# Start addresses of TensorE's operands in SBUF, one encoder layer on one core

## The chip, the cores and the metric

The kernel runs on one core of a Trainium2 chip. The metric is the device time of one launch in microseconds (us); lower is better. Engines are named as in the profile: PE is TensorE's matmul, PEld its weight load, DVE is VectorE, ACT is ScalarE, SP issues the DMAs.

## The reference

One layer of an encoder on 512 tokens with 1024 features, float32. With `rms` for a normalization over the features with a gain, it computes

```
h = x + 0.5 * rms(ffn1(rms(x)))          ffn(u) = (silu(u @ Wg) * (u @ Wu)) @ Wd, inner size 2816
h = h + rms(mixer(rms(h)))               mixer: w_in -> q, k, v, pool, two gates; attention over a
                                         neighbourhood of an 8 x 64 grid, pooling with four windows,
                                         each projected, gated and added, then w_out
h = h + 0.5 * rms(ffn2(rms(h)))
h = h + rms((p @ Wp) * sigmoid(rms(h) @ Wgate))
```

## The kernel before

Features lie on the 128 partitions and tokens along the row, so an activation is eight tiles of 128 x 512. Every float32 value is kept as a high part rounded to fp32r and a low remainder. `mm3` makes one product of a 128 x 128 weight block out of three matmuls: high weight by high activation (L277), high weight by low activation (L278), low weight by high activation (L279). In each, the weight block is the stationary operand (read by PEld) and the activation the moving one.

Weights arrive in chunks of 128 x 1024 words (class `Stream`). A chunk is loaded by SP into a ring of five `raw` tiles, split by ACT (high part, L243) and DVE (low part, L165) into one of six `w` tiles, and freed when PE has used it. `pump` works up to `SPLIT_AHEAD` = 4 chunks ahead. A `w` tile is 2176 words wide, 128 more than its two halves need, so that the halves can begin at a shift, in words, that depends on the kind of the chunk (`self.shift`); the low half lies 1088 words behind the high one, which is a multiple of 256 bytes. `plan()` gives the kind: 0 for products of 512 columns, 1 for groups that are done in two halves of 256 tokens (first and last groups of a stage, so that norms can overlap), 2 for quads.

A quad (`fast_group`) makes two row blocks of gate and up projections with seven products of half size in place of eight, each of 24 matmuls with 256 columns, into three PSUM banks p, q and r. Product i takes its moving operands from `moving(i, k)`: products 0, 1 and 6 from the normalized input `uh`, `ul`, products 3 and 4 from the combined inputs x0 to x3, products 2 and 5 from x4 to x7. `xtile(n)` says where the combined input n is kept: x0 to x3 in the tiles of tag y, x4 and x5 in tags pth and ptl, x6 and x7 in tag e. Each of the two FFNs has three parts (`PARTS`): a first part with groups 0 to 2 in 512 columns, and two parts of four quads; each part ends with its down projection. So there are four stages of four quads.

The order of instructions is written out by hand: a list of Python generators with due times (`Clock`, `TIMES`) places norms, attention and pooling between the matmuls. The change touches none of these times.

Tiles lie one behind another in each pool, every row rounded up to 32 bytes, and tags in the order of their first use; that is why some tags are taken once, early, with nothing written. In the memory map of the compiled program the starts modulo 256 bytes are:

```
tiles                                                       pool    start mod 256
h, uh, ul, acc, rb, and tags f, y, zh0, zh1, zl0, zl1       act     0
rc_pre (16 bytes)                                           tmp     0
pth, ptl, e                                                 tmp     32
w tiles (six, 8704 bytes each)                              wsp     0; operands at 4 x shift:
    kind 0                                                          0
    kind 1, and quads but for i = 2, 5                              64
    quads, i = 2, 5                                                 96
```

All offsets inside these tiles at which a matmul begins are multiples of 256 bytes.

Of the kernel before, what the change touches and what calls it, by code (L numbers as in the profile page):

```python
# [10 lines left out]
F32 = mybir.dt.float32  # L11
F32R = mybir.dt.float32r
# [3 lines left out]
P = 128  # L16
S = 512
# [4 lines left out]
NT = 4  # L22
# [96 lines left out]
def kernel(  # L119
# [16 lines left out]
    act = ctx.enter_context(tc.tile_pool(name="act", bufs=1))  # L136
    tmp = ctx.enter_context(tc.tile_pool(name="tmp", bufs=2))
# [33 lines left out]
    class Stream:  # L171
# [5 lines left out]
        def __init__(self):  # L177
            self.ops = []
            self.needs = []
            self.shift = []  # L180
            chunk = 0
            for kind in plan():
                quad = kind == 2
                for i in range(7 if quad else 1):
                    self.ops.append((quad, chunk, i))
                    self.needs.append(chunk + (self.LOADS[i] if quad else 1))
                    self.shift.append(24 if quad and i in (2, 5) else 16 if kind else 0)
                chunk += 4 if quad else 1
            self.n = len(self.ops)
            assert chunk == n_chunks  # L190
            self.loaded = 0
            self.split = 0
            self.done = 0
            self.hold = False
            self.freed = set()
            self.over = set()
            self.raw = {}
            self.parts = {}
            self.both = None
# [95 lines left out]
    G1PRE, G1POST, GMPRE, GMPOST, G2PRE, G2POST, GPPRE, GPPOST = (gain(v) for v in range(8))  # L295
    pscale = [g_sb[:, 64 + g:65 + g] for g in range(4)]

    h = [act.tile([P, S], F32, name=f"h{k}") for k in range(KD)]
    uh = [act.tile([P, S], F32R, name=f"uh{k}") for k in range(KD)]
    ul = [act.tile([P, S], F32R, name=f"ul{k}") for k in range(KD)]  # L300
    acc = act.tile([P, S], F32, name="acc")
    rb = act.tile([P, S], F32, name="rb")

    rc_pre = tmp.tile([P, NT], F32, name="rc_pre", bufs=1)
    for tag, bufs in (("pth", 2), ("ptl", 2), ("e", 4)):
        tmp.tile([P, S], F32, tag=tag, name=tag, bufs=bufs)

    def u_rhs(k):
        return uh[k], ul[k]
# [191 lines left out]
    def ffn(chains, gpre, gpost, gnext):  # L501
# [21 lines left out]
        def combined():  # L523

            for k in range(4):
                a, b = un[k], un[k + 4]
                tt(a[:, LEFT], a[:, LEFT], a[:, RIGHT], ALU.subtract)
                tt(a[:, RIGHT], a[:, RIGHT], b[:, RIGHT], ALU.subtract)
                stt(b[:, RIGHT], a[:, LEFT], -1.0, b[:, RIGHT], ALU.mult, ALU.subtract)
                tt(b[:, LEFT], b[:, LEFT], b[:, RIGHT], ALU.add)  # L530
                for n, src in ((k, a), (k + 4, b)):
                    xh[n], xl[n] = xtile(n)
                    nc.scalar.copy(xh[n], src)
                    tt(xl[n], src, f32(xh[n]), ALU.subtract)
                yield TIMES["comb"]

        def xtile(n):
            if n < 4:
                return [act.tile([P, S], F32R, tag="y", name="x", bufs=8) for _ in range(2)]
            if n < 6:  # L540
                return [tmp.tile([P, S], F32R, tag=t, name="x") for t in ("pth", "ptl")]
            return [tmp.tile([P, S], F32R, tag="e", name="x", bufs=4) for _ in range(2)]

        def moving(i, k):
# [505 lines left out]
def plan():  # L1050

    def ffn(first):
        out = []
        for g0, g1 in PARTS:
            for g in range(g0, g1):
                out += [2] if g in FAST else [first if g == 0 else 0] * 4
            out += [0] * (g1 - g0) + [int(g1 == PARTS[-1][1])] * (g1 - g0)
        return out

    mixer = [1] * 4 + [0] * (3 * 4 + 1 + 16 + 8 + 4) + [1] * 4  # L1060
    return ffn(0) + mixer + ffn(1) + [0] * 3 + [1] * 8
# [114 lines left out]
```

## Time and profile before

| | |
|---|---|
| median of three runs | 1081.99 us (1080.77 to 1083.11) |
| the profiled execution | 1084.12 us, its span 1082.3 us |
| PE busy | 1060.2 us, 6762 matmuls |
| DVE busy, ACT busy | 762.3 us, 544.2 us |
| HBM read | 104.93 MB |

The span is the time from the first to the last instruction of one profiled execution; the execution's own time holds a little more at both ends. A matmul's duration in a row includes its way through the array and overlaps the next one's, so the pace of a run of matmuls is read from one start to the next.

### The profile page before, as it was taken

The numbers are of one execution on the slowest core, as the hardware profiler recorded it, in microseconds if no ns is written. First come the engines' busy times: TensorE is split into PE (matmuls) and PEld (weight loads), VectorE is DVE, ScalarE is ACT, GpSimd is POOL, SyncE is SP. The second block draws the span as 40 slices with busy tenths as digits, with TensorE's granted clock in tenths as the row PEclk, the third lists the DMA queues.
The fourth block names the chain that finished last, engine by engine and source line by source line (L and its number), as shares of the span: only waits on it lengthen the run. The fifth ranks groups of instructions, "written<-read, shape, count | busy, mean of one in ns | idle before, by whom it ended". The sixth has DMA issues, their size and how long they took to land.

```text
span 1082.3 us, 16827 instructions
## 1 busy us (share of the span) xinstructions
PE 1060.2 (98%) x6762; PEld 955.9 (88%) x6762; DVE 762.3 (70%) x1279; ACT 544.2 (50%) x921; POOL 0.7 (0%) x6
## 2 busy tenths in 40 slices
PE   9999999999999999999999999999999999999994
PEld 7788999889999988877888899888999889999894
DVE  7893787558854987977444429994787558854976
ACT  8552555235543765366222247752555235543874
POOL 0000000000000000000000000000000000000000
PEclk9999999999999999999999999999999999999997
DMA  8331335223362342231333321342235223341202
GB/s 297 107 104 59 87 109 157 78 78 104 111 178 50 108 153 79 78 98 45 99 96 95 97 76 40 107 133 72 81 115 155 79 79 100 109 162 60 63 17 79
DMA packets 37023, 108.12 MB, mean 100 GB/s; under 512 B 4816, under 2 KB 11472, under 8 KB 36944
## 3 DMA queue, kind: packets, MB, share of 16 engines
q1 hardware_dynamic: 36800, 107.01, 31.7%
q8 instruction: 53, 0.87, 0.3%
q14 instruction: 26, 0.21, 0.1%
q10 hardware_dynamic: 144, 0.03, 0.0%
HBM read 104.93 MB, written 2.10 MB: 99 GB/s over the span
## 4 chain that ended last, share of the span: by engine, by line
PE 90%; DVE 6%; ACT 3%; issue 0%; DMA 0%; DVEq 0%; ACTq 0%
PE g L277 14%; PE g L278 14%; PE g L279 14%; PE p L278 6%; PE p L279 6%; PE p L277 6%; PE r L278 3%; PE r L279 3%; PE r L277 3%; PE gate L279 2%; PE gate L277 2%; PE gate L278 2%; PE q L278 1%; PE q L279 1%; PE q L277 1%; PE br L277 1%
## 5 line engine op out<-in xcount | busy, mean ns | idle before, releaser
L165 DVE TENSOR_TENSOR w<-raw,w 128x1024 fp32r<-128x1024 f32 (+1 forms) x227 | 273.7, 1208 | 152.6 <-ACT w L243 152.4
L243 ACT CAST w<-raw 128x1024 fp32r<-128x1024 f32 (+1 forms) x227 | 234.7, 1038 | 262.1 <-PE g L279 131.5
L277 PE MATMUL g<-zh,w 128*128 128x512 f32 (+1 forms) x512 | 178.6, 349 | 0.0
L278 PE MATMUL g<-zl,w 128*128 128x512 f32 (+1 forms) x512 | 178.3, 348 | 0.0
L279 PE MATMUL g<-zh,w 128*128 128x512 f32 (+1 forms) x512 | 178.3, 348 | 0.0
L279 PE MATMUL g<-uh,w 128*128 128x256 f32 (+1 forms) x448 | 146.5, 330 | 1.4 <-DVE w L165 1.4
L278 PE MATMUL g<-ul,w 128*128 128x256 f32 (+1 forms) x448 | 147.4, 330 | 0.2 <-DVE ul L168 0.2
L277 PE MATMUL g<-uh,w 128*128 128x256 f32 (+1 forms) x448 | 146.4, 331 | 0.6 <-ACT w L243 0.6
L278 PEld LDWEIGHTS g<-zl,w 128*128 128x128 f32 x512 | 96.6, 189 | 12.4
L279 PEld LDWEIGHTS g<-zh,w 128*128 128x128 f32 x512 | 96.2, 188 | 12.6
L277 PEld LDWEIGHTS g<-zh,w 128*128 128x128 f32 x512 | 96.2, 188 | 12.4
L279 PEld LDWEIGHTS g<-uh,w 128*128 128x128 f32 x448 | 84.7, 190 | 9.7 <-DVE w L165 1.6
L278 PEld LDWEIGHTS g<-ul,w 128*128 128x128 f32 x448 | 85.4, 191 | 8.5 <-DVE ul L168 0.6
L277 PEld LDWEIGHTS g<-uh,w 128*128 128x128 f32 x448 | 84.8, 190 | 8.8 <-ACT w L243 0.9
L279 PE MATMUL p<-uh,w 128*128 128x256 f32 x256 | 71.9, 281 | 0.0
L278 PE MATMUL p<-ul,w 128*128 128x256 f32 x256 | 71.9, 281 | 0.0
L277 PE MATMUL p<-uh,w 128*128 128x256 f32 x256 | 71.9, 281 | 0.0
L278 PE MATMUL p<-x,w 128*128 128x256 f32 x256 | 71.5, 279 | 0.0
L278 PE MATMUL r<-x,w 128*128 128x256 f32 x256 | 71.5, 279 | 0.0
L279 PE MATMUL p<-x,w 128*128 128x256 f32 x256 | 71.5, 279 | 0.0
L279 PE MATMUL r<-x,w 128*128 128x256 f32 x256 | 71.4, 279 | 0.0
L277 PE MATMUL p<-x,w 128*128 128x256 f32 x256 | 71.4, 279 | 0.0
(195 smaller groups left out, 2187.6 us busy)
## 6 DMA issues: line engine op xcount, KB each, us to landing
raw<-in_wst SPq DMA_DIRECT2D x191, 512.0 KB, 3.6
h<-in_x SPq DMA_DIRECT2D x8, 256.0 KB, 5.5
bm<-in_bias SPq DMA_DIRECT2D x64, 32.0 KB, 2.2
out<-o SPq DMA_DIRECT2D x16, 128.0 KB, 1.7
raw<-in_wst SPq DMA_DIRECT2D x4, 128.0 KB, 4.0
g_sb<-in_gains ACTq DMA_DIRECT2D x1, 34.0 KB, 3.2
edge_sb<-in_edge SPq DMA_DIRECT2D x1, 32.0 KB, 5.3
```

Source lines behind the costliest of these rows:

```text
L165: nc.vector.tensor_tensor(o, a, b, op=op)
L243: nc.scalar.copy(hi[:, sl], raw[:, sl])
L277: nc.tensor.matmul(o, wh, xh, start=first, stop=False, **kw)
L278: nc.tensor.matmul(o, wh, xl, start=False, stop=False, **kw)
L279: nc.tensor.matmul(o, wl, xh, start=False, stop=last, **kw)
```

## The change

`rc_pre` moves from the pool tmp to the front of the pool act, where it takes eight words of a row. The early taking of tags in tmp is put in another order, with 56 words of padding ahead of pth. Both tiles of the combined input x4 are taken from tag pth, both of x5 from ptl. The shift of a weight chunk is 24 words for kinds 1 and 2 and 8 words for kind 0.

```diff
@@ class Stream, __init__
-                    self.shift.append(24 if quad and i in (2, 5) else 16 if kind else 0)
+                    self.shift.append(24 if kind else 8)
@@ tile_encoder_kernel
+    rc_pre = act.tile([P, 8], F32, name="rc_pre")[:, 0:NT]
     h = [act.tile([P, S], F32, name=f"h{k}") for k in range(KD)]
     uh = [act.tile([P, S], F32R, name=f"uh{k}") for k in range(KD)]
     ul = [act.tile([P, S], F32R, name=f"ul{k}") for k in range(KD)]
     acc = act.tile([P, S], F32, name="acc")
     rb = act.tile([P, S], F32, name="rb")
-
-    rc_pre = tmp.tile([P, NT], F32, name="rc_pre", bufs=1)
-    for tag, bufs in (("pth", 2), ("ptl", 2), ("e", 4)):
+    for tag, bufs in (("ptl", 2), ("e", 4)):
         tmp.tile([P, S], F32, tag=tag, name=tag, bufs=bufs)
+    tmp.tile([P, 56], F32, name="pad", bufs=1)
+    tmp.tile([P, S], F32, tag="pth", name="pth")
@@ ffn, xtile
             if n < 6:
-                return [tmp.tile([P, S], F32R, tag=t, name="x") for t in ("pth", "ptl")]
+                return [tmp.tile([P, S], F32R, tag="pth" if n == 4 else "ptl", name="x") for _ in range(2)]
```

## Rows read from the trace of the kernel before

**Rows 1.** The page's head and busy times: span, busy us, share, instructions.
```profile
span 1082.3 us, 16827 instructions
...
PE 1060.2 (98%) x6762; PEld 955.9 (88%) x6762; DVE 762.3 (70%) x1279; ACT 544.2 (50%) x921; POOL 0.7 (0%) x6
```

**Rows 2.** The page's chain that ended last, shares by engine.
```profile
PE 90%; DVE 6%; ACT 3%; issue 0%; DMA 0%; DVEq 0%; ACTq 0%
```

**Rows 3.** Stretches: length, busy of PE, PEld, DVE, ACT, POOL; clock, DMA, GB/s.
```profile
110.40:188.80 78.40, 78.40 (x673) 78.40 (x672) 62.29 (x71) 43.89 (x63) 0.00 (x0) 1.00 0.40 120
188.80:232.40 43.60, 43.60 (x194) 36.11 (x194) 21.67 (x24) 9.72 (x11) 0.00 (x0) 1.00 0.24 75
...
882.50:961.00 78.50, 78.50 (x674) 78.46 (x673) 64.16 (x74) 43.23 (x61) 0.00 (x0) 1.00 0.38 121
```

**Rows 4.** The same view, the first quad's products 0 to 3.
```profile
110.34:113.17 2.83, 2.83 (x25) 2.82 (x24) 1.05 (x1) 1.65 (x3) 0.00 (x0) 1.00 0.00 0
113.17:116.00 2.83, 2.83 (x26) 2.83 (x25) 1.22 (x2) 1.53 (x2) 0.00 (x0) 1.00 0.51 143
116.00:118.74 2.74, 2.74 (x26) 2.74 (x25) 2.27 (x4) 1.37 (x2) 0.00 (x0) 1.00 0.60 194
118.74:121.57 2.83, 2.83 (x26) 2.83 (x25) 2.34 (x3) 1.54 (x2) 0.00 (x0) 1.00 0.10 39
```

**Rows 5.** PE in order of time, product 2: start us, duration us, instruction.
```profile
116.01 0.28 PE L277 MATMUL p<-x,w 128*128 128x256 f32 x1
116.12 0.29 PE L278 MATMUL p<-x,w 128*128 128x256 f32 x1
116.25 0.28 PE L279 MATMUL p<-x,w 128*128 128x256 f32 x1
116.37 0.28 PE L277 MATMUL p<-x,w 128*128 128x256 f32 x1
...
118.63 0.28 PE L279 MATMUL p<-x,w 128*128 128x256 f32 x1
```

**Rows 6.** PE in order of time, two half groups, first and last of 97 and 39.
```profile
332.70 0.28 PE L277 MATMUL g<-zh,w 128*128 128x256 f32 x1
...
344.00 0.28 PE L277 MATMUL g<-zh,w 128*128 128x256 f32 x1
...
355.93 0.28 PE L277 MATMUL g<-uh,w 128*128 128x256 f32 x1
...
360.23 0.28 PE L279 MATMUL g<-uh,w 128*128 128x256 f32 x1
```

**Rows 7.** PE in order of time, a down projection: its begin, and later.
```profile
188.86 0.40 PE L277 MATMUL g<-zh,w 128*128 128x512 f32 x1
...
190.25 0.39 PE L277 MATMUL g<-zh,w 128*128 128x512 f32 x1
...
199.77 0.39 PE L277 MATMUL g<-zh,w 128*128 128x512 f32 x1
...
201.81 0.39 PE L277 MATMUL g<-zh,w 128*128 128x512 f32 x1
```

**Rows 8.** PE in order of time, the matmuls of pool_map and the next.
```profile
449.57 0.40 PE L277 MATMUL py<-ph,w 128*128 128x512 f32 x1
...
450.27 0.39 PE L277 MATMUL g<-uh,w 128*128 128x512 f32 x1
```

**Rows 9.** Groups by line and shape, 110.40 to 188.80, the split of weights.
```profile
L165 DVE TENSOR_TENSOR w<-raw,w 128x1024 fp32r<-128x1024 f32 x25 | 30.6, 1224 | 13.8 <-ACT w L243 13.8
L243 ACT CAST w<-raw 128x1024 fp32r<-128x1024 f32 x25 | 26.2, 1050 | 11.9 <-PE p L279 5.2 <-PE q L279 3.9 <-issue 2.8
```

**Rows 10.** DMA issues: KB each, median us from issue to landing.
```profile
h<-in_x SPq DMA_DIRECT2D x8, 256.0 KB, 5.5
```

## The prediction, made before the change was run

> **What bounds the kernel now.** I read the page's busy times first: TensorE (PE) is busy 98% of the 1082.3 us span and the next engine, DVE, 70% [rows 1]. The chain of work that ended last says the same from the other end: 90% of it is PE [rows 2]. So a matmul that starts sooner after the one before it shortens the run, unless something else then becomes late. The view of stretches shows where PE never stops: in a quad stage (four quads, rows at 110.40 and 882.50) PE is busy for the whole length, at a granted clock of 1.00 (2.4 GHz), with DVE at 62 to 64 and ACT at 43 to 44 of 78.5 us [rows 3]; a down projection of 512-column products (188.80) is equally full. There PE waits for nobody, so the only thing that can change is the pace of back-to-back matmuls.
>
> The pace is not the printed duration of a matmul (it includes the pipeline); it is the distance from start to start. For that I took the four products of the first quad as stretches [rows 4]. The products that begin at 110.34, 113.17 and 118.74 take 2.83 us per 24 matmuls, 117.8 ns each; the one that begins at 116.00 takes 2.74, though it has the same 24 matmuls of 256 columns. Its single starts [rows 5]: 116.01 to 116.12, 116.25, 116.37 is 0.36 us for three, still slow; from 116.37 to 118.63 there are 20 steps in 2.26 us, 113 ns each. I followed all 16 quads: every product of index 2 or 5 begins with three slow steps and then runs at 113 to 114, and every other product runs at 117.8 throughout. The fast pace is 17/16 of 256 columns at 2.4 GHz (106.7 ns), 113.3 ns.
>
> What is different in products 2 and 5 is in the code: their weights are at shift 24 words (96 bytes modulo 256) and their moving operands are x4 to x7 in the tiles pth, ptl and e, which lie at 32; all others have weights at 64 and moving operands at 0. The distance, 64 bytes, is the same in both pairs. So (weights 96, moving 32) has so far always ended in the fast pace, and (64, 0) in a quad always in the slow one.
>
> One more group of rows warns against reading this as a law of addresses [rows 6]. The half groups have (64, 0) too. The one that starts at 332.70, straight after 512-column products, runs 96 steps in 11.30 us, 117.7 ns. But the 38 steps from 355.93 take 4.30 us, 113.2 ns, at the same addresses, after PE had been interrupted for a norm. Both paces can hold at (64, 0); which one holds depends also on how the stretch was entered.
>
> **The change part by part.** rc_pre becomes the first tile of act and takes 32 bytes there, so h, uh, ul, acc, rb and all the y, f, zh and zl tiles move from 0 to 32. Its 32 bytes leave tmp, so ptl and e stay at 32; 224 bytes of padding put pth at 0. Weights of kinds 1 and 2 go to 96, those of kind 0 to 32. xtile gives x4 both pth buffers (0) and x5 both ptl buffers (32), where each had one of each: the same four buffers, all read for the last time in the same product, so no new wait. No instruction is added, removed or moved in the program's order. What changes is the address pair of nearly every matmul:
>
> Quads, moving operand other than x4: (96, 32), the pair that was fast. 16 quads × 5 products go from 24 × 117.8 = 2.827 to 24 × 113.3 = 2.720 us: 80 × 0.107 = −8.5 us. The 32 products of index 2 and 5 took 2.742; without their slow entry −0.022 each, −0.7. As a cross-check, a quad stage has 672 matmuls in 78.4 us, 116.7 ns each [rows 3]; four stages × 672 × 3.35 ns above 113.3 are 9.0 us, about the two terms together. If the first two products of a stage, entered from 512-column products, keep the slow pace as 332.70 did, 4 stages × 2 × 0.107 = 0.86 us of it is lost; bounds 0 and 0.86, I take +0.4.
>
> x4: its three matmuls come first in each column block of products 2 and 5, 16 × 2 × 2 = 64 places, now at (96, 0), a pair no stretch of the trace holds. From below they run at 113.3, cost 0; from above each place costs what the entry of product 2 costs, three steps of 0.36 us against 0.34 [rows 5], 21 ns unrounded, 64 × 21 = 1.35 us. Nothing shows a gain. I take the middle, +0.7.
>
> Half groups: 1,344 matmuls from (64, 0) to (96, 32). Summed over all their steps they lie 3.8 us above 113.3. If entry decides, nothing is gained; if the addresses do, 3.8. I take −1.2, nearer to nothing because the longest slow stretch was entered from 512 columns, which stays so.
>
> 512-column products: 2,364 matmuls from (0, 0) to (32, 32). They run at 226.7 ns (9 steps from 199.77 to 201.81 take 2.04 us) [rows 7], which is per column exactly the fast pace of the quads, 2 × 113.3; I see no faster pace per column anywhere, which excludes a gain. A loss is not excluded: the only 512-column matmuls with an offset between their operands, the three of pool_map with weights at 0 and moving at 32, take 0.70 us [rows 8], 233 ns, and 2,364 × 6.3 would be +15 us. There the distance changed as well; in the change it stays 0. I take 0.
>
> ACT, DVE and DMA: the split of a weight chunk takes ACT 1.05 and DVE 1.22 us [rows 9], 2.27 against a product of 2.72, and DVE stays near 64/78.5 × 1.04 = 85% in a quad stage, so weights still arrive in time; were this cover gone, PE would wait for w, 0.1 us per product at most since that is all the product shrinks. The eight loads of h (256 KB, 5.5 us each to landing [rows 10]) now write at 32 modulo 256; between nothing and a tenth of the last one's landing, 0 to 0.5 us, I take +0.2.
>
> Sum: −8.5 − 0.7 + 0.4 + 0.7 − 1.2 + 0 + 0.2 = −9.1 us. The profiled execution took 1084.1 (span 1082.3), so 1075.0; it lies 2.1 above the median of the runs shown, 1082.0, so the forecast for the median is 1072.9, say **1073**.
>
> **A rule that speaks against it.** The same matmul, 256 columns at full clock, has a start-to-start of 117.8 in one product and 113.3 in the next [rows 4, 5]. The Trainium skill, page "TensorE: Matmul & The Clock Gate", section "Step-by-step: what each phase is for", says PE has two independent SBUF read ports, so that loading the next weights takes nothing from the running matmul; by that no pair of addresses would matter and the change would be worth 0. This trace does not agree as far as the two paces go, but the rule could still hold for addresses if only the entry sets the pace.
>
> **The rivals.**
> No effect: the pace is set by what interrupted PE last, not by addresses, and half of the interruptions stay. For it: both paces at one pair [rows 6]. Against it: 32 of 32 entries into (96, 32) turned fast. About 1082, between 1080 and 1084.
>
> Slower, the border: the flip to fast comes from the step of the offset itself (weights 96 meet one last moving operand at 0), and the flip back from the step down. With one pair everywhere the borders vanish, quads entered from 512 columns stay slow as at 332.70, and products 2 and 5 lose their gain: 32 × (2.827 − 2.742) = +2.7, with x4 up to +1.3 more: 1085. It decides if x4's own step up does not flip the pace. Against it: x4 at 0 beside weights at 96 is just that step up, once in product 2 of the first quad.
>
> Half: x4's steps flip the pace to and fro, and half of all 112 quad products are slow: 56 × 0.107 = 6.0 us above the fast pace, plus 1.0 for the steps, where it is now 9.3: −2.3, 1080.
>
> Slower, 512 columns: they lose their lock. At 3.8 ns each (9.1 / 2364) the gain is gone; at pool_map's pace, −9.1 + 15 = +6, 1088. Against it: their distance stays 0, and after they start off slow behind a quad stage (6 steps in 1.39 us, 232 ns, from 188.86) they come back to 226.7 [rows 7].
>
> **How the numbers follow.** Forecast (most quad products at 113 to 114, 512 columns unchanged) 0.62; half 0.12; no effect 0.06; border 0.12; 512 columns slower 0.08. A measurement of this kernel can tell about 0.2%, 2.2 us, from no change. Faster by that: 0.62 and most of the half case, 0.70. Within it: no effect and the rest of half, 0.13. Slower: border and most of the 512 case, 0.17. The forecast's own range is 1069 (all of the half groups gained, nothing lost: −13.0) to 1077 (all losses at their bounds, no half groups). The range for 8 in 10 goes from 1068 to 1085, through half and no effect up to the border case.
>
> **What would show it.** In the profile after: the product stretches of a quad at 2.72 to 2.74 us instead of 2.83; a quad stage of four at about 76 us instead of 78.5; matmul rows p, q and r at 276 ns where they were 281; 512-column steps still 226 to 227. Wrong would be: quad products other than 2 and 5 still at 117 to 118 (border or no effect), fast and slow products in turn (half), 512-column steps of 230 or more, or a wait of PE on w inside a quad stage.

## The result and the profile after

The changed kernel takes 1076.96 us (median of seven runs, 1074.13 to 1078.02) against 1083.11 (1080.77 to 1085.73) before: the medians lie 6.15 us apart, and the ratio of the runs is 0.9934, 95% interval 0.9921 to 0.9946, about 7 us. The forecast was 1073 within 1068 to 1085.

The page's head, busy times and chain after the change, which answer to [rows 1, 2]:

```profile
span 1076.2 us, 16825 instructions
...
PE 1054.3 (98%) x6762; PEld 950.6 (88%) x6762; DVE 760.6 (71%) x1279; ACT 544.4 (51%) x921; POOL 0.7 (0%) x6
...
PE 94%; DVE 3%; ACT 2%; DMA 0%; issue 0%; DVEq 0%; ACTq 0%
```

Still 6762 matmuls, still PE as the bound; PE is busy 5.9 us less. The view of stretches says where. First the four quad stages, from the first matmul of each to the first one behind it (columns as in rows 3):

```profile
110.11:186.84 76.73, 76.73 (x673) 76.72 (x672) 61.70 (x71) 43.98 (x63) 0.00 (x0) 1.00 0.41 123
230.39:307.12 76.73, 76.73 (x674) 76.73 (x672) 63.52 (x74) 43.37 (x61) 0.00 (x0) 1.00 0.42 125
756.69:833.42 76.73, 76.73 (x673) 76.72 (x672) 61.70 (x71) 43.98 (x63) 0.00 (x0) 1.00 0.41 123
876.97:953.69 76.72, 76.72 (x673) 76.72 (x672) 63.50 (x74) 43.37 (x61) 0.00 (x0) 1.00 0.41 123
```

76.7 us each where it was 78.4 to 78.5 [rows 3]: from start to start the 2,688 quad matmuls took 314.0 us before and take 306.9 now, 7.1 less, about the whole gain. PE waits for nothing in there. Before, the quads lay 9.4 us above the fast pace (2,688 steps of 113.3 ns), now they lie 2.3 above it. Now the products of the first two quads of the first stage, 0 to 3 of each (compare rows 4):

```profile
110.11:112.94 2.83, 2.83 (x25) 2.82 (x24) 1.06 (x1) 1.65 (x3) 0.00 (x0) 1.00 0.00 0
112.94:115.77 2.83, 2.83 (x27) 2.83 (x25) 1.23 (x2) 1.53 (x2) 0.00 (x0) 1.00 0.41 146
115.77:118.56 2.79, 2.79 (x26) 2.79 (x25) 2.32 (x4) 1.37 (x2) 0.00 (x0) 1.00 0.61 185
118.56:121.28 2.72, 2.72 (x26) 2.72 (x25) 2.19 (x3) 1.53 (x2) 0.00 (x0) 1.00 0.11 44
...
129.48:132.20 2.72, 2.72 (x26) 2.72 (x25) 2.72 (x5) 2.28 (x4) 0.00 (x0) 1.00 0.16 63
132.20:134.92 2.72, 2.72 (x26) 2.72 (x25) 2.72 (x4) 1.73 (x3) 0.00 (x0) 1.00 0.35 69
134.92:137.68 2.76, 2.76 (x26) 2.76 (x25) 2.76 (x4) 1.47 (x2) 0.00 (x0) 1.00 0.60 184
137.68:140.40 2.72, 2.72 (x26) 2.72 (x25) 2.21 (x3) 1.53 (x2) 0.00 (x0) 1.00 0.35 136
```

Products 0 and 1 of the first quad have the pair (96, 32), the one that was fast, and run at the slow pace, 2.83. Product 2 begins slow, and the rest of the stage is fast, 2.72; products with x4 take 2.76. The single starts of product 2 show the place of the flip, in its second block, right behind x4's three matmuls at 117.18, 117.30 and 117.42. The first block begins with the same three, at 115.77, and behind them the pace stays slow: from 116.12 to 117.18 there are 9 steps in 1.06 us, 118 ns.

```profile
115.77 0.28 PE L277 MATMUL p<-x,w 128*128 128x256 f32 x1
...
116.12 0.28 PE L277 MATMUL p<-x,w 128*128 128x256 f32 x1
...
117.18 0.28 PE L277 MATMUL p<-x,w 128*128 128x256 f32 x1
117.30 0.28 PE L278 MATMUL p<-x,w 128*128 128x256 f32 x1
117.42 0.28 PE L279 MATMUL p<-x,w 128*128 128x256 f32 x1
117.54 0.28 PE L277 MATMUL p<-x,w 128*128 128x256 f32 x1
117.65 0.28 PE L278 MATMUL p<-x,w 128*128 128x256 f32 x1
117.77 0.28 PE L279 MATMUL p<-x,w 128*128 128x256 f32 x1
...
118.45 0.28 PE L279 MATMUL p<-x,w 128*128 128x256 f32 x1
```

From 117.54 to 118.45 there are 8 steps in 0.91 us, 114 ns. The other three stages do the same at the same place.

Outside the quads the paces are as before. 512-column products are at 226.7 ns as in rows 7, within the rounding of these two rows (7 steps in 1.58 us):

```profile
198.43 0.39 PE L277 MATMUL g<-zh,w 128*128 128x512 f32 x1
...
200.01 0.39 PE L278 MATMUL g<-zl,w 128*128 128x512 f32 x1
```

The half groups lie 3.8 us above the fast pace, as before, and the loads of h still land in 5.5 us. One thing is new in this execution: the granted clock falls once more than in the one before. Stretches around one wait of PE in the last stage, after:

```profile
1012.00:1015.90 3.90, 2.45 (x21) 2.23 (x20) 3.70 (x10) 3.55 (x9) 0.00 (x0) 1.00 0.00 0
1015.90:1019.30 3.40, 3.40 (x17) 3.40 (x18) 3.02 (x7) 2.30 (x6) 0.00 (x0) 0.50 0.50 154
1019.30:1023.00 3.70, 3.70 (x34) 3.70 (x34) 3.53 (x8) 1.00 (x3) 0.00 (x0) 1.00 0.40 142
```

and before:

```profile
1018.00:1022.00 4.00, 3.87 (x33) 3.63 (x31) 3.80 (x12) 3.67 (x12) 0.00 (x0) 1.00 0.00 0
1022.00:1025.40 3.40, 2.08 (x17) 2.06 (x18) 3.38 (x9) 3.40 (x8) 0.00 (x0) 1.00 0.26 64
1025.40:1029.00 3.60, 3.60 (x33) 3.56 (x32) 3.60 (x6) 1.00 (x3) 0.00 (x0) 1.00 0.52 198
```

The matmul behind the wait, after and before (in brackets the wait and what ended it):

```profile
1015.76 0.72 PE L279 MATMUL g<-uh,w 128*128 128x256 f32 x2 [1.45 <-DVE w L165]
```

```profile
1023.32 0.39 PE L279 MATMUL g<-uh,w 128*128 128x256 f32 x1 [1.45 <-DVE w L165]
```

In both, PE waits 1.45 us for a weight split; after it the granted clock fell to 0.50 (1.2 GHz) for 3.4 us in the changed kernel, which costs half of that, 1.7 us, and not in the other. Runs with a mean granted clock of 0.994 took 1074.1 to 1074.7 us, those at 0.991 took 1077.7 to 1078.0; before, in the first comparisons, 0.994 went with 1080.7 to 1082.4 and 0.991 with 1085.5 to 1085.7. At equal clock the medians of these runs differ by 6.6 us (0.994) and 7.6 us (0.991), about the quads' 7.1.

### The profile page after: what moved, and what is told of

The parts are those of the page before. It is cut to its first block, busy times and chain, and to the rows that moved or that the text cites. A ratio compares the mean times of both kernels' runs of the same rounds, so it can differ in the third digit from the quotient of the medians.

```text
span 1076.2 us, 16825 instructions
## 1 busy us (share of the span) xinstructions
PE 1054.3 (98%) x6762; PEld 950.6 (88%) x6762; DVE 760.6 (71%) x1279; ACT 544.4 (51%) x921; POOL 0.7 (0%) x6
## 4 chain that ended last, share of the span: by engine, by line
PE 94%; DVE 3%; ACT 2%; DMA 0%; issue 0%; DVEq 0%; ACTq 0%
PE g L277 15%; PE g L279 15%; PE g L278 15%; PE p L278 5%; PE p L277 5%; PE p L279 5%; PE r L277 3%; PE r L278 3%; PE r L279 3%; PE gate L279 2%; PE gate L278 2%; PE gate L277 2%; PE q L277 1%; PE q L278 1%; PE q L279 1%; PE br L279 1%
```

## The experiments

Diffs are against the changed kernel unless another is named. "Distance" is the start of the weights minus the start of the moving operand, modulo 256 bytes.

**Is the pair (96, 32) fast, or did x4's step make it so?** x4 goes to 32 like the rest:

```diff
-    for tag, bufs in (("ptl", 2), ("e", 4)):
+    for tag, bufs in (("ptl", 2), ("e", 4), ("pth", 2)):
         tmp.tile([P, S], F32, tag=tag, name=tag, bufs=bufs)
     tmp.tile([P, 56], F32, name="pad", bufs=1)
-    tmp.tile([P, S], F32, tag="pth", name="pth")
```

> The changed kernel, but with pth at 32 too, so that x4 has the pair (96, 32) like every other operand of a quad; the padding stands behind pth. Border theory (only the distance of weights to moving operand counts, 64 bytes here as before, and a step of the distance from 64 to 96 is what flips the slow pace to the fast one): no step is left in a quad stage, so all 112 quad products keep the slow pace they get from the 512-column products, 2.83 us each, 12.0 us above the fast pace where the kernel before had 9.4 and the changed one 2.3: +2.6 us against before, about 1085.5. Address theory (the pair (96, 32) is fast once PE has been on it for a while): the products turn fast without the step, and without x4's cost of about 1.3 us: 1074 to 1076.

Measured: 1086.61 us against 1083.03, 1.0035 (1.0022 to 1.0048): slower than before. Two of its quad stages:

```profile
108.04:187.19 79.15, 79.15 (x674) 79.15 (x672) 62.36 (x71) 43.80 (x63) 0.00 (x0) 1.00 0.39 120
230.73:309.88 79.15, 79.15 (x673) 79.14 (x672) 64.18 (x74) 43.23 (x61) 0.00 (x0) 1.00 0.40 120
```

79.15 / 672 is 117.8 ns: all 2,688 quad matmuls are slow, at the pair that was fast in the kernel before. The address theory, that the pair as such is fast, falls; the loss of 2.6 us that the border theory gives is what the quads lost (314.0 to 316.6).

**Do the addresses count at all?** Everything 32 bytes lower, all distances kept:

```diff
-                    self.shift.append(24 if kind else 8)
+                    self.shift.append(16 if kind else 0)
...
-    rc_pre = act.tile([P, 8], F32, name="rc_pre")[:, 0:NT]
...
     tmp.tile([P, S], F32, tag="pth", name="pth")
+    rc_pre = tmp.tile([P, NT], F32, name="rc_pre", bufs=1)
```

> The changed kernel with every operand 32 bytes lower: activations at 0, weights of kinds 1 and 2 at 64, of kind 0 at 0, ptl and e at 0, pth (x4) at 224. All distances and steps are those of the changed kernel, all addresses but x4's are those of before. Border theory: the same as the changed kernel, -6 to -7 us against before, 1075 to 1077, quad products 2.72 to 2.77 us but for the first two of a stage. Address theory: (64, 0) is the slow pair, so quad products at 2.83 us, 1083 to 1086.

Measured: 1077.05 us, 0.9943 (0.9927 to 0.9959), and the first stage:

```profile
110.57:187.29 76.72, 76.72 (x673) 76.72 (x672) 61.70 (x71) 43.94 (x63) 0.00 (x0) 1.00 0.41 123
```

The same 76.7 us as in the changed kernel, at the pair (64, 0) that was slow before. Moving everything by 32 bytes is worth nothing. The run without x4's step was slow and this one, with it, is fast: the gain is x4's step.

**The pace at every distance.** As the first experiment, with

```diff
-                    self.shift.append(24 if kind else 8)
+                    n = sum(o[0] == quad for o in self.ops) - 1
+                    self.shift.append((8 + 4 * (n // 7)) % 64 if quad else 24 if kind else (8 + 4 * (n // 2)) % 64)
```

> No forecast of the time: a measurement of the pace by distance. As the first run (all activations and x at 32), but each of the 16 quads has another shift, so that the distance of weights to moving operand goes from 0 to 240 bytes in steps of 16, quad by quad; 512-column chunks go through the same distances two chunks at a time. Border theory: paces at distance 64 are the two known, others may have one pace each, 113 to 118; the 512-column pace is 226.7 at distance 0 and may differ elsewhere (233 in pool_map at 224). Address theory: only the quad at (96, 32) is fast.

and the same downwards, 512 columns at distance 0:

```diff
+                    self.shift.append((4 - 4 * (n // 7)) % 64 if quad else 24 if kind else 8)
```

> A measurement of the pace, not of the time: as the scan before, quads at distances 240, 224 down to 0, in that order, every border between two quads a step down of 16 bytes (the scan before went up); 512-column weights at distance 0. Border theory: at distance 64, entered from 80, the fast pace of 113.3 where the scan up, entered from 512 columns, had 117.8; at distances with one pace only, the same numbers as in the scan up (116.7 at 208 and 224, 120.0 at 0, 144 and 240). If the direction of the step plays no part: the same numbers everywhere, 117.8 at 64.

Mean step in ns of products 1 to 6 of each quad, worked out from the starts in the two traces:

```
distance   0    16    32    48    64    80    96   112   128   144   160   176   192   208   224   240
up     120.0 118.3 118.3 117.8 117.8 118.8 118.7 120.0 118.7 120.0 120.0 118.1 117.8 116.7 116.7 120.0
down   120.0 118.3 118.3 118.3 113.3 118.7 118.7 120.0 118.7 116.7 120.0 118.1 117.8 116.7 117.8 117.3
```

(One run each: 1099.33 us up, 1087.29 down.) The quad at distance 64, entered from a down projection in the scan up and from distance 80 in the scan down:

```profile
237.41:257.20 19.79, 19.79 (x169) 19.78 (x168) 15.68 (x19) 9.74 (x13) 0.00 (x0) 1.00 0.35 106
```

```profile
821.12:840.17 19.05, 19.05 (x170) 19.05 (x169) 13.01 (x17) 11.07 (x16) 0.00 (x0) 1.00 0.55 165
```

So 113.3 appeared at distance 64 alone, and there it depends on the entry. Distances 48, 144, 224 and 240 also had two paces, and my expectation that 144, 224 and 240 have one was wrong.

512-column products kept 226.7 at distances 0 and 240 and mostly at 16, and ran at about 230 to 234 elsewhere. Two chunks of 24 matmuls in the scan up, at distance 224 (233 ns) and at 240 (227 ns):

```profile
728.02:733.62 5.60, 5.60 (x25) 4.50 (x24) 5.15 (x11) 3.23 (x5) 0.00 (x0) 1.00 0.01 3
739.08:744.52 5.44, 5.44 (x25) 4.51 (x24) 5.07 (x7) 2.32 (x4) 0.00 (x0) 1.00 0.61 205
```

From start to start they lost 10.7 us against the kernel before and the quads 4.7, which together make most of the 16 us by which the scan up was slower.

The Trainium skill, page "TensorE: Matmul & The Clock Gate", section "Step-by-step: what each phase is for", says that the two operands come over independent read ports, so that loading the next weights takes nothing from the running matmul. For this stream of fp32r products the measurement decides against what follows from it, that no distance would matter: 256 columns took from 113.3 to 120.0 ns by distance and entry.

**A step at the begin of a stage, and only there.** One pair everywhere, as in the first experiment, but the weights of the first product of a stage at 128:

```diff
-                    self.shift.append(24 if kind else 8)
+                    first = quad and i == 0 and not self.ops[-2][0]
+                    self.shift.append(32 if first else 24 if kind else 8)
```

> As the first run (one pair everywhere), but the weights of the first product of each quad stage lie at 128, so that its 24 matmuls have the distance 96, and then 64 again. Border theory: this step, at the begin of each stage and only there, flips the pace; after product 0 (24 steps of about 118) all products of the stage run at 113.3, so the quads lie 4 x 0.11 = 0.4 us above the fast pace where the changed kernel has 2.3: 1.8 us below the changed kernel, about 8.9 below before, 1074. Address theory: (96, 32) is fast by itself from product 1 on, the same time; the first run tells the two apart. If the step must be short (one to three matmuls) to flip the pace, all products stay at 2.83: 1085.

Measured: 1074.88 us, 0.9920 (0.9904 to 0.9936). Products 0 and 1, and the stage:

```profile
109.90:112.72 2.82, 2.82 (x26) 2.82 (x25) 1.06 (x1) 1.63 (x3) 0.00 (x0) 1.00 0.00 0
112.72:115.44 2.72, 2.72 (x26) 2.72 (x25) 1.12 (x2) 1.54 (x2) 0.00 (x0) 1.00 0.53 142
...
109.90:186.16 76.26, 76.26 (x673) 76.26 (x672) 61.72 (x71) 43.84 (x63) 0.00 (x0) 1.00 0.42 123
```

Product 0 is slow, and in the whole stage the quads lie 0.1 us above the fast pace; four stages × (76.73 − 76.26) are 1.9 us less than in the changed kernel, as expected.

**Does the side matter from which the distance comes back to 64?** The same, with 16 in place of 32 in the last line, so that product 0 has distance 32:

> As the kernel with the step in the first product of each quad stage, but with that product's weights at 64, distance 32, so that the distance comes to 64 from below. If only a return from above flips the pace (in the kernel before, the step from 32 back to 64 went with the flip to slow): product 0 at 118.3, all others at 117.8, about 1086. If any step flips it: product 1 on at 113.3, about 1075.

Measured: 1073.10 us against 1083.61, 0.9901 (0.9885 to 0.9916):

```profile
107.97:110.81 2.84, 2.84 (x26) 2.84 (x24) 1.07 (x1) 1.63 (x3) 0.00 (x0) 1.00 0.00 0
110.81:113.53 2.72, 2.72 (x27) 2.72 (x25) 1.10 (x2) 1.53 (x2) 0.00 (x0) 1.00 0.54 134
```

The quad stages take 76.28 us each, as with the step from above. The side does not matter for these two. That took away the direction, which I had read from the kernel before (up flips to fast, down to slow).

**The same step for the half groups.**

```diff
-            chunk = 0
+            chunk = halves = 0
...
-                    self.shift.append(24 if kind else 8)
+                    halves += kind == 1
+                    first = halves % 4 == 1 if kind == 1 else quad and i == 0 and not self.ops[-2][0]
+                    self.shift.append(32 if first else 24 if kind else 8)
```

> As the kernel with the step in the first product of each quad stage, and the same step (weights at 128) in the first chunk of each group that is done in halves. Border theory: the half groups fall into the fast pace behind each such chunk; of their 3.5 us above the fast pace a third or more goes, 1 to 2 us below the kernel with the step in the quads alone, 1073 to 1074. If norms in between set the half groups back at once, or the chunk's own slow steps (336 of 1,344 matmuls at 118.7) eat it: no difference, 1075.

Measured: 1075.14 us, 0.9912 (0.9897 to 0.9928), no better than without it; the half groups lie 4.2 us above the fast pace, where the kernel without their step had 3.5. In the first half group behind a down projection, the chunk with the step and the rest of the block:

```profile
328.38:329.08 0.70, 0.70 (x7) 0.70 (x6) 0.70 (x2) 0.70 (x2) 0.00 (x0) 1.00 0.23 47
329.08:331.20 2.12, 2.12 (x20) 2.12 (x19) 2.12 (x4) 1.60 (x3) 0.00 (x0) 1.00 0.28 55
```

2.12 us for 18 matmuls is 117.8 ns each: the return from six matmuls at distance 96 did not flip the pace there. So not every step does it.

**The change and the two steps side by side** on one chip:

> The changed kernel, beside the next two on one chip. Quads 2.3 us above the fast pace, as in its first trace: 0.993 to 0.994 of before, 1076 to 1077.

> The step from above in the first product of each quad stage (weights at 128), once more. Quads 0.4 us above the fast pace, 1.9 less than in the changed kernel: 0.992 of before, about 1075.

> The step from below (weights at 64), once more. Its quads took the same as with the step from above, so the same time, about 1075; the 1.8 us by which it was faster in the earlier run then came from elsewhere. If it is faster again by over 1 us, the half groups or the start are to be looked at.

Measured against 1083.07 us: the change 1078.57, 0.9956 (0.9943 to 0.9968); the step from above 1074.52, 0.9919 (0.9906 to 0.9933); from below 1074.33, 0.9919 (0.9906 to 0.9933). The change missed its expected 1076 to 1077; its quads took 306.9 us again. Either step is about 4 us faster than the change: 1.9 us from the quads, and the rest fits the granted clock, which was 0.991 in all five runs of the change here and 0.992 to 0.994 in those of the two steps. Between the first 10 and the last 20 us of the profiled executions the clock fell to 0.50 twice in the change, at 33.1 and 1016.2, once with the step from above and not at all with the step from below. Stretches of the change, then of the step from above, then of the step from below:

```profile
33.10:36.50 3.40, 3.40 (x10) 2.68 (x9) 2.08 (x4) 0.38 (x1) 0.00 (x0) 0.50 0.47 154
1016.20:1019.60 3.40, 3.40 (x18) 3.40 (x18) 2.98 (x7) 2.29 (x5) 0.00 (x0) 0.50 0.56 154
```

```profile
33.00:36.40 3.40, 3.40 (x10) 2.71 (x9) 2.11 (x4) 0.38 (x1) 0.00 (x0) 0.50 0.52 154
1015.90:1019.30 3.40, 3.40 (x31) 3.32 (x30) 3.40 (x6) 1.03 (x3) 0.00 (x0) 1.00 0.57 182
```

```profile
33.00:36.40 3.40, 3.40 (x16) 2.77 (x16) 2.98 (x5) 1.89 (x3) 0.00 (x0) 1.00 0.40 145
```

At 1.7 us a fall, the quads and the clock together give 3.6 and 5.3 us; the spans of these executions were 3.2 and 5.7 shorter. What makes the clock fall in one kernel and not in another was not tested. The 1.8 us between the two steps in the earlier runs did not come back in their medians. These are the fastest versions found.

## Why the prediction was right, and where not

**The bound** was read rightly: PE's pace in the quad stages, with cover by ACT and DVE enough (no wait of PE in a stage).

**Quads, −8.5 and −0.7, less 0.4 for the entry and 0.7 for x4: −8.1 expected, −7.1 measured.** The sizes of the two paces were right. The reason given for −8.5, "(96, 32), the pair that was fast", failed: at one pair everywhere all quads are slow, and 32 bytes lower they are as fast. What acts is the mechanism that stood among the rivals as the border, with the event that it named as its own limit, x4's step. The prediction had the step as a cost of +0.7 and the rival at 0.12. That the time came near the forecast is luck in this: without the step the same kernel took 1086.61 us. The step acted only in the second block of product 2: both of the first two products and most of the third stay slow, 4 × (0.11 + 0.11 + 0.07) = 1.2 us, where I had bounds of 0 and 0.86 for two products. x4 costs 2.76 − 2.72 = 0.04 us in each of the other 28 products that hold it, 1.1 us, near the upper bound of 1.35 and not the middle. The two together are 2.3 us above the fast pace, 1.2 more than the 0.4 and 0.7 with which I had counted. Against that, the quads before lay 9.4 us above it, and not the 9.2 of the two gain terms: 1.0 us less gain than expected.

**Half groups, −1.2:** 0. Their pace at one pair of addresses differs with the entry and with what interrupts them, as rows 6 had shown (117.7 from 332.70, 113.2 from 355.93), and the change takes away neither.

**512 columns, 0:** right, and for the reason given: their distance stayed 0. The scan up shows that the bound of +15 us was real: at most other distances they run at about 233.

**DMA, +0.2:** the median landing of h is 5.5 us in both. In a second profiled execution of the change it is 6.0, so a shift of the size that the term allows could not have been seen.

**Sum:** −9.1 expected, −6.1 in the profiled span and about −7 by the runs of equal clock. The 2 us between come from half groups (1.2) and quads (1.0), less the 0.2 of the DMA term; the profiled execution lost 1.7 us more to the fall of the clock. The upper end of the forecast's own range, 1077, does not follow from its terms: all losses at their bounds and no half groups give −6.5 us, so 1075.5 from the median of 1082.0, and the measured 1076.96 lies above that.

**The rule of independent ports** was rightly given little weight. No steady stretch of this stream came below 113.3 ns for 256 columns and 226.7 for 512, 17/16 of the bare columns at 2.4 GHz. The Trainium skill, page "TensorE: Matmul & The Clock Gate", section "Step-by-step: what each phase is for", gives the gap of back-to-back matmuls as columns / 2.4 GHz and about 2.5 ns, 216 ns for 512 columns, and 109 for 256 as an estimate by the same sum; the traces here do not agree.

Open: what in the hardware makes 113.3 hold or not. The runs show that the distance of the two operands decides which paces there are and that an entry chooses among them. They do not show which entries flip it, since 24 matmuls at distance 32 or 96 did, three at 96 did in the second block of product 2 and not in the first, and six in the half group did not, nor why the same 1.45 us wait of PE is followed by half clock in one kernel and not in the other.

## What to carry to other kernels

Where a back-to-back matmul stream is the bound, measure its step from start to start, not its duration, and look whether the same shape has two of them. The distance of weights and moving operand modulo 256 bytes is a choice worth a scan (in this fp32r stream 113.3 to 120.0 ns for 256 columns, 226.7 to about 234 for 512), but a pace read at one address pair must be tried with another entry before it is put down to the address. Moving all operands together by 32 bytes changed nothing here, so try padding where it changes a distance.

## What was unexpected of the hardware

At distance 64 a stream of 256-column fp32r matmuls, each with its own weight load, holds either 113.3 or 117.8 ns per matmul for a whole stage (672 matmuls at the slow pace, 648 at the fast one). A single product of 24 at distance 32 or 96, ahead of it, settles it at 113.3 for the rest of the stage in all eight stages of the first two traces with that step (four with each). Of the 16 distances of the two scans none other had a pace under 116.7.
